# Twelve units of the conditioning matrix at another place in a transformer layer on one core

## The chip, the cores and the metric

The kernel runs on one core of a Trainium2 chip. The metric is the device time of one execution, in microseconds (us). TensorE multiplies matrices, VectorE, ScalarE and GpSimd work element by element, and SyncE's queue starts nearly all transfers from the chip's memory (HBM) to the core's memory (SBUF). In the profile's rows TensorE is PE (PEld its loads of weights), VectorE DVE, ScalarE ACT, GpSimd POOL, and SyncE's queue SPq.

## The reference

One layer of an encoder with three mixers, 256 tokens of 2048 features, in fp32. What matters here is where the conditioning vector enters:

```python
mod = silu(c) @ ada_w + ada_b                       # (2048) @ (2048, 6*2048)
sh1, sc1, gt1, sh2, sc2, gt2 = split(mod, 6)
h = rms(x, norm1_g) * (1 + sc1) + sh1
na.., da.., gd.. = split_cols(h @ w_in)             # inputs of three mixers -> ya, yb, yc
gates = sigmoid(h @ gate_w + gate_b)                # three gates of 2048 columns
merged = gates0 * (ya @ w_branch_a) + gates1 * (yb @ w_branch_b) + gates2 * (yc @ w_branch_c)
x = x + gt1 * (merged @ w_out)
h2 = rms(x, norm2_g) * (1 + sc2) + sh2
x = x + gt2 * ((silu(h2 @ ffn_w1) * (h2 @ ffn_w3)) @ ffn_w2)
```

ya is a neighbourhood attention, yb a differential attention, yc a gated delta rule.

## The kernel before

**The weight stream.** All weights of the large products pass through the core once, as 128x128 tiles in one list that stream_plan writes (line 58). Eight tiles, 128x1024 numbers or 512 KB, are one transfer (load, L929) and are called a half; there are 538 halves. A half is split into a high and a low part of reduced mantissa: ScalarE casts the raw weights to `wh`, and VectorE writes `wl` = raw - wh (conv, L948). The matrix engine then makes wh times both parts of the activations and wl times the high part. The order of the stages is: the input projection, gate A and branch A, gate B with branch B, gate C (halves 194 to 225), branch C, the output projection (from half 242), the feed-forward part (from half 274).

**The units.** mod is computed on VectorE, not on TensorE. Its matrix, transposed, comes in 192 units of 512 KB (ada_units, L254): one transfer into a tile of the pool `raw`, and one scalar_tensor_tensor that multiplies it with silu(c), broadcast in `sb`, and sums along the row into one column of `part`. In the rows a unit's tile is `araw`. Weights and units share the pool `raw` of six buffers, and both kinds of transfer are issued in one order on SyncE's queue. A unit's buffer is free when VectorE has used it, a weight buffer when VectorE has written wl.

**The order of the work.** A loop over the halves (L1154) carries out the units hooked to a half, splits up to two halves ahead (LA = 2), loads up to four ahead, issues the half's matmuls and, after the last one of each tile, advances the side work (the attentions and the delta rule, run_side at L908). Within that order a scheduler of the language's library settles the order of each engine's queue and which buffer a tile gets, when the kernel is built. After the start of the kernel nothing else pins the order on VectorE and ScalarE (`pin` at L153).

**Where the units go.** The first 96 units make shift1 and scale1 and are spread over the input projection. The next 96, called the middle units here, make gate1, shift2 and scale2, 32 for each. They are spread evenly, in order, over three stretches of halves by lines 1129 to 1132, with two borders from line 31:

```python
ADA_AT, ADA_MID = 9, (64, 84)
...
rest = [u for i in range(3) for u in ada_units(ns + i)]
spread(rest[:ADA_MID[0]], first[("ga", ADA_AT)], first[("gc", 0)])
spread(rest[ADA_MID[0]:ADA_MID[1]], first[("gc", 0)], first[("pc", 0)])
spread(rest[ADA_MID[1]:], first[("out", 0)], first[("out", 12)])
```

`first` gives the half in which a group of tiles begins. Worked out from stream_plan these borders are half 132 (the tenth group of gate A), 194, 226, and 242 to 266 of the output projection. The last 32 units (gate2) lie in the feed-forward part.

Of the kernel before, what the change touches and what calls it, by code (L numbers as in the profile page):

```python
# [27 lines left out]
ORDERS = [ALT, [(0, 0), (1, 0), (0, 1), (1, 1)] + ALT[4:], [(0, 0), (0, 1), (1, 1), (1, 0)] + ALT[4:]]  # L28

SHORT = 8  # L30
ADA_AT, ADA_MID = 9, (64, 84)

W = dict(col=4, tok=3, kn=6, s=2, sm=12, sm2=22, pt=5, av=3, gs=21, gt=5, dec=3, prep=3, a=8, x0=9,
         l1=8, l2=6, l3=10, kv=18, uu=6, sw=5, so=6, go=2, conv=2, z=9, sqn=8, pgn=1, sqd=8, pgd=2,
# [1281 lines left out]
```

## Time and profile before

| | us |
|---|---|
| median of 3 runs | 1729.36 (1725.44 to 1732.31) |
| the profiled execution's own time | 1725.35 |
| its span, first to last instruction | 1723.6 |
| TensorE busy in the span | 1697.6 |
| VectorE busy | 1261.2 |
| ScalarE busy | 850.4 |

The span is the part of the execution that the trace shows; the rest, 1.75 us, lies around it. An engine that is busy has an instruction in execution; a matmul's end is modelled in the profile.

### The profile page before, as it was taken

Reading aid. Unit: us, or ns where it says so; the run is one execution under the profiler, and the core shown is the slowest. Engines: PE = TensorE matmul, PEld = TensorE weight load, DVE = VectorE, ACT = ScalarE, POOL = GpSimd, SP = SyncE. Lnnn points to the kernel's source line nnn. Section 1 sums busy time; section 2 is a strip of 40 time slices with the busy share of each in tenths; the row PEclk is TensorE's granted clock in tenths of the full one; section 3 lists DMA queues with packets and bytes.
Section 4 is the critical chain, followed back from the end, with each engine's and each line's share of the span. In section 5 each row is a group of like instructions: output and inputs, shape, how many; then the busy total and the mean of one; then the engine's idle time right before and its main releaser. Section 6 shows DMA issues by size and latency. Waiting matters only on the chain.

```text
span 1723.6 us, 27955 instructions
## 1 busy us (share of the span) xinstructions
PE 1697.6 (98%) x10988; PEld 1531.2 (89%) x10988; DVE 1261.2 (73%) x1895; ACT 850.4 (49%) x1249; POOL 39.1 (2%) x25
## 2 busy tenths in 40 slices
PE   8999999999999999999999999999999999999999
PEld 6999999998889898899898788888888888888887
DVE  6898777986999899876878776666666666545454
ACT  4454455666673445334745554444444444443433
POOL 0000000000003100300000000000000000000000
PEclk9999999999999999999999999999999999999999
DMA  8999964553587775766768567666666666666662
GB/s 326 333 357 324 341 207 156 180 187 128 194 291 237 246 267 195 254 209 214 252 222 278 168 208 227 225 229 224 227 226 229 224 225 226 196 196 202 196 201 96
DMA packets 109432, 393.12 MB, mean 228 GB/s; under 512 B 12146, under 2 KB 14450, under 8 KB 109300
## 3 DMA queue, kind: packets, MB, share of 16 engines
q1 hardware_dynamic: 106852, 389.08, 67.1%
q10 hardware_dynamic: 2448, 2.25, 0.4%
q8 instruction: 86, 1.41, 0.3%
q14 instruction: 46, 0.38, 0.1%
HBM read 389.19 MB, written 2.10 MB: 227 GB/s over the span
## 4 chain that ended last, share of the span: by engine, by line
PE 56%; DVE 1%; DMA 1%; ACT 0%; issue 0%; ACTq 0%; DVEq 0%
PE mm L166 54%; PE sd L166 2%; DMA araw<-ada 1%; DVE wl L157 0%; PE sd L169 0%; ACT wh L157 0%; ACT of L157 0%; DVE araw L157 0%; DVE gc L157 0%; DVE x L157 0%; DVE m L157 0%; DVE po L157 0%; DVE p L157 0%; ACT sq L157 0%; ACT p L157 0%
## 5 line engine op out<-in xcount | busy, mean ns | idle before, releaser
L157 DVE TENSOR_TENSOR wl<-raw,wh 128x1024 fp32r<-128x1024 f32 x538 | 662.8, 1233 | 316.7 <-ACT wh L157 314.1
L157 ACT CAST wh<-raw 128x1024 fp32r<-128x1024 f32 x538 | 563.6, 1048 | 636.1 <-PE mm L166 339.5
L166 PE MATMUL mm<-hp,wh 128*128 128x256 f32 (+1 forms) x2336 | 572.8, 328 | 5.7 <-ACT hp L157 3.2
L166 PE MATMUL mm<-h,wh 128*128 128x512 f32 x1408 | 486.6, 393 | 0.0
L166 PE MATMUL mm<-hp,wl 128*128 128x256 f32 x1552 | 423.3, 282 | 0.0
L166 PEld LDWEIGHTS mm<-hp,wh 128*128 128x128 f32 x2336 | 383.6, 191 | 35.8 <-issue 7.4
L166 PE MATMUL mm<-h,wl 128*128 128x256 f32 x1408 | 387.6, 279 | 0.0
L166 PEld LDWEIGHTS mm<-h,wh 128*128 128x128 f32 x1408 | 261.7, 187 | 57.5 <-DVE sl L157 0.3
L166 PEld LDWEIGHTS mm<-hp,wl 128*128 128x128 f32 x1552 | 295.4, 190 | 12.2 <-issue 3.9
L157 DVE SCALAR_TENSOR_TENSOR araw<-araw,sb 128x1024 f32<-128x1024 f32 x192 | 237.0, 1239 | 86.9 <-DMA araw<-ada 86.3
L166 PEld LDWEIGHTS mm<-h,wl 128*128 128x128 f32 x1408 | 265.1, 188 | 2.6
L166 PE MATMUL mm<-hid,wh 128*128 128x512 f32 x704 | 243.2, 392 | 0.0
L166 PE MATMUL mm<-hid,wl 128*128 128x256 f32 x704 | 193.8, 279 | 0.0
L166 PEld LDWEIGHTS mm<-hid,wh 128*128 128x128 f32 x704 | 130.8, 187 | 28.5
L166 PEld LDWEIGHTS mm<-hid,wl 128*128 128x128 f32 x704 | 132.6, 188 | 1.3
L166 PE MATMUL mm<-m,wh 128*128 128x512 f32 x256 | 89.7, 397 | 0.4 <-DVE po L157 0.3
L166 PE MATMUL mm<-m,wl 128*128 128x256 f32 x256 | 70.8, 280 | 0.0
L166 PEld LDWEIGHTS mm<-m,wh 128*128 128x128 f32 x256 | 47.7, 188 | 12.0 <-DVE po L157 0.6
L758 POOL TENSOR_TENSOR X<-X,of 128x512 f32<-128x512 f32 x20 | 38.4, 1930 | 705.8 <-ACT of L157 705.5
L166 PE MATMUL sd<-hp,wh 128*128 128x256 f32 x256 | 49.5, 283 | 0.0
L166 PEld LDWEIGHTS mm<-m,wl 128*128 128x128 f32 x256 | 48.3, 189 | 0.5
L166 PE MATMUL mm<-yc,wh 128*128 128x256 f32 x256 | 46.2, 283 | 0.0
(251 smaller groups left out, 1521.4 us busy)
## 6 DMA issues: line engine op xcount, KB each, us to landing
raw<-wst SPq DMA_DIRECT2D x538, 512.0 KB, 4.3
araw<-ada SPq DMA_DIRECT2D x192, 512.0 KB, 4.4
x<-xT SPq DMA_DIRECT2D x8, 512.0 KB, 7.1
out<-x ACTq DMA_DIRECT2D x16, 128.0 KB, 3.9
nab<-nab SPq DMA_DIRECT2D x2, 512.0 KB, 6.8
cst<-cst SPq DMA_DIRECT2D x1, 896.0 KB
vec<-vec ACTq DMA_DIRECT2D x1, 152.0 KB, 2.3
lam<-lamv SPq DMA_DIRECT2D x1, 128.0 KB, 3.4
```

The costliest lines, as they stand in the source:

```text
L157: i = f(*a, **k)
L166: return chain("pe", nc.tensor.matmul(*a, **k))
L758: nc.gpsimd.tensor_tensor(sel(X, b), sel(X, b), nat(of[:], b), op=ALU.subtract)
```

## The change

The two borders in the list of the middle units become 52 and 78. The first stretch (halves 132 to 193) has 52 units in place of 64, the third gate (194 to 225) 26 in place of 20, the output projection (242 to 265) 18 in place of 12. Twelve units move later, and every unit keeps its place in the order of units.

```diff
-ADA_AT, ADA_MID = 9, (64, 84)
+ADA_AT, ADA_MID = 9, (52, 78)
```

## Rows read from the trace of the kernel before

**Rows 1.** The page: busy us of each engine, and the group of casts.
```profile
PE 1697.6 (98%) x10988; PEld 1531.2 (89%) x10988; DVE 1261.2 (73%) x1895; ACT 850.4 (49%) x1249; POOL 39.1 (2%) x25
...
L157 ACT CAST wh<-raw 128x1024 fp32r<-128x1024 f32 x538 | 563.6, 1048 | 636.1 <-PE mm L166 339.5
```

**Rows 2.** Busy by stretch: length, PE, PEld, DVE, ACT, POOL, clock, DMA share, GB/s.
```profile
100.00:205.00 105.00, 105.00 (x877) 105.00 (x876) 90.41 (x146) 52.41 (x84) 0.00 (x0) 1.00 0.93 330
435.00:710.00 275.00, 267.74 (x1829) 242.11 (x1828) 253.77 (x397) 143.04 (x229) 28.47 (x14) 1.00 0.72 243
710.00:835.00 125.00, 123.89 (x805) 110.38 (x804) 91.62 (x130) 56.52 (x77) 9.88 (x6) 1.00 0.66 217
883.00:951.00 68.00, 67.55 (x392) 58.76 (x391) 55.99 (x90) 33.61 (x48) 0.00 (x0) 1.00 0.82 270
```

**Rows 3.** Waits of TensorE, 435 to 710 us: us in total, times, longest.
```profile
PE sd L166 <- DVE Y L157: 3.2, 3, 1.7
PE sd L169 <- DVE q L157: 2.4, 1, 2.4
PE sd L169 <- DVE a L157: 1.1, 1, 1.1
```

**Rows 4.** Groups of VectorE, 435 to 710 us: busy, mean ns, idle before.
```profile
L157 DVE SCALAR_TENSOR_TENSOR araw<-araw,sb 128x1024 f32<-128x1024 f32 x64 | 81.1, 1267 | 17.5 <-DMA araw<-ada 17.3
```

**Rows 5.** Groups of VectorE, 710 to 835 us.
```profile
L157 DVE SCALAR_TENSOR_TENSOR araw<-araw,sb 128x1024 f32<-128x1024 f32 x20 | 24.7, 1234 | 19.4 <-DMA araw<-ada 19.3
```

**Rows 6.** Waits of VectorE, 883 to 951 us.
```profile
DVE araw L157 <- DMA araw<-ada: 6.9, 8, 1.2
DVE wl L157 <- ACT wh L157: 5.7, 7, 1.5
```

**Rows 7.** Timeline of SyncE's queue, 900 to 915 us: start, duration.
```profile
908.27 0.33 SPq L260 DMA_DIRECT2D araw<-ada  x1
...
914.21 0.33 SPq L260 DMA_DIRECT2D araw<-ada  x1
```

**Rows 8.** Timeline of VectorE, 900 to 915 us.
```profile
907.01 1.23 DVE L157 SCALAR_TENSOR_TENSOR araw<-araw,sb 128x1024 f32<-128x1024 f32 x1 [0.86 <-DMA araw<-ada]
908.16 0.08 DVE L157 DVE_READ_ACCUMULATOR araw<-araw,sb 128x1 f32 x1
...
912.95 1.23 DVE L157 SCALAR_TENSOR_TENSOR araw<-araw,sb 128x1024 f32<-128x1024 f32 x1 [0.31 <-DMA araw<-ada]
```

**Rows 9.** Timeline of SyncE's queue, 476 to 488 us.
```profile
483.71 0.33 SPq L260 DMA_DIRECT2D araw<-ada  x1
```

**Rows 10.** Timeline of VectorE, 476 to 492 us.
```profile
482.45 1.22 DVE L157 SCALAR_TENSOR_TENSOR araw<-araw,sb 128x1024 f32<-128x1024 f32 x1
...
484.91 1.23 DVE L157 SCALAR_TENSOR_TENSOR araw<-araw,sb 128x1024 f32<-128x1024 f32 x1
...
488.14 1.23 DVE L157 SCALAR_TENSOR_TENSOR araw<-araw,sb 128x1024 f32<-128x1024 f32 x1 [0.86 <-DMA araw<-ada]
```

**Rows 11.** The chain that ended last, 895 to 915 us: start, us, what.
```profile
901.85 5.06 DMA araw<-ada
...
908.24 1.14 DVE wl L157
...
909.76 5.44 PE mm L166 x29
```

**Rows 12.** Groups of VectorE, 100 to 205 us.
```profile
L157 DVE SCALAR_TENSOR_TENSOR araw<-araw,sb 128x1024 f32<-128x1024 f32 x29 | 35.4, 1220 | 0.5 <-DMA araw<-ada 0.5
```

**Rows 13.** Transfers, 100 to 205 us: count, KB each, median us to landing.
```profile
araw<-ada SPq DMA_DIRECT2D x28, 512.0 KB, 5.2
```

**Rows 14.** Transfers, 883 to 951 us.
```profile
araw<-ada SPq DMA_DIRECT2D x11, 512.0 KB, 4.4
```

**Rows 15.** Timeline of VectorE, 949 to 952 and 983 to 986 us.
```profile
950.35 0.17 DVE L157 SCALAR_TENSOR_TENSOR G<-mod,vec 128x16 f32<-128x16 f32 x1
...
984.11 1.27 DVE L157 SCALAR_TENSOR_TENSOR ht<-x,G,rstd 128x256 f32<-128x256 f32 x3
```

## The prediction

> **What bounds the kernel now.** I read first the page's busy times: TensorE works 1697.6 us of a span of 1723.6 us [rows 1]. A change that moves VectorE work and transfers can win only what TensorE stands idle, 26.0 us in all, and only the part of it that lies where work is taken away. So the second view is the busy time by stretch, cut where the change cuts [rows 2]. I took the borders from the order of VectorE's wl writes (one for each block of eight weight tiles, called a half here): the first gates and first two branches (halves 132 to 193) run from 435 to 710 us, the third gate (194 to 225) from 710 to 835 us, and the first 24 halves of the output projection (242 to 265) from 883 to 951 us. TensorE's idle time is 275.00 - 267.74 = 7.26 us in the first, 125.00 - 123.89 = 1.11 us in the second, and 68.00 - 67.55 = 0.45 us in the third. The granted clock is at its upper level (1.00 in the rows, 2.4 GHz) in all of them.
>
> Third, what those idle times wait for. In the first stretch nearly all is TensorE standing at a matmul of the side chains for VectorE's Y, q and a: 3.2 + 2.4 + 1.1 us [rows 3]. VectorE is the engine that is late there: 253.77 us busy and 17.3 us waiting at a unit for its transfer, 98.6% of the 275 us [rows 2, 4]. In the third gate it is 91.62 + 19.3 of 125, 88.7% [rows 2, 5]. In the projection it has 6.9 us of waits for units and 5.7 us for casts [rows 6].
>
> Fourth, how a unit travels, in the queues themselves. In the projection a unit's load is issued at 908.27, just after the unit before it has been used (907.01 + 1.23), and the next again at 914.21, just after 912.95 + 1.23 [rows 7, 8]: one buffer goes round, and a unit costs load plus use. In the first gates, with a unit for nearly every half, two go round: the load at 483.71 follows the use at 482.45 and feeds the use at 488.14, with the one at 484.91 between them [rows 9, 10]. The chain that ended last passes in the projection through such a load (901.85, 5.06 us) and reaches TensorE at 909.76 [rows 11]. So there the units already set the pace at places, with almost no idle time to show for it.
>
> **The change part by part.** A unit is one transfer of 512 KB on SyncE's queue (issue 0.33 us [rows 7]) and one multiply-and-sum on VectorE, 1.22 to 1.27 us, with a read of the accumulator of 0.08 us behind it, beside which the next instruction starts [rows 8]. The change leaves all 192 of them, their order and their deadlines; 12 leave the first gates (64 to 52), 6 more come to the third gate (20 to 26, over 32 halves) and 6 more to the projection (12 to 18, over 24 halves). No work of TensorE, ScalarE or GpSimd is added or removed.
>
> *First gates, a gain.* VectorE loses 12 x (1.267 + 17.3/64) = 18.4 us [rows 4], 6.7 points of 275 us. What TensorE's idle time does with it, I read between the two gate stretches, which have the same kinds of work: 2.64% idle at 98.6% occupation against 0.89% at 88.7%, 0.177 points for one. At 91.9% that is 2.64 - 1.19 = 1.45%, 4.0 us in place of 7.26: **-3.3 us**. The ends are 0 (the stalls are set by the order of the side chains, not by the load) and -7.3 us (all of them go). SyncE's queue has 12 issues less, and the weights' loads behind them come earlier, which nobody waits for.
>
> *Third gate, a small loss.* Six units more are 6 x 1.234 = 7.4 us, 5.9 points, so by the same slope +1.05 points of 125 us: **+1.3 us**. If each new unit also waits as the present ones do (19.3/20 = 0.97 us [rows 5]), it is 13.2 us, 10.6 points, +2.3 us; the lower end is 0, since VectorE waits there 19.3 us at the units themselves and new work could lie in that time. I take 1.3, because a wait for a unit was shorter, 0.27 us, where the units were denser [rows 4]. Behind a waiting unit stand the wl write of the next half and the evacuation of a gate tile; TensorE waits for these only when they are later than the two halves that are split ahead.
>
> *Projection, a loss.* VectorE waits 12.6 us of 68, so 55.4 us are taken [rows 6]. Six units more, at 1.15 us from one start to the next instruction's, are 6.9 us. If each of the 18 waits 6.9/12 = 0.58 us for its transfer as the 12 do now, that is 10.4 us; in all 55.4 + 6.9 + 10.4 = 72.7 us, 4.7 us more than the stretch has. Some of it is lent by the halves split ahead: 392 matmuls in 67.55 us make a half of 16 matmuls 2.76 us [rows 2]; two halves less one cast and one wl write (1.05 and 1.23 us [rows 1]) are 3.2 us. As the chain is already at TensorE in this stretch [rows 11], I count half of that as free: 4.7 - 1.6 = **+3.1 us**. The lower end is 0: from 100 to 205 us the kernel has 29 units in 105 us, one per 3.6 us, as many as the projection would have (18 in the 24 x 2.76 = 66 us of its halves, one per 3.7 us), and VectorE waits only 0.5 us for them and TensorE never stands [rows 2, 12]. The upper end is the rival below, +8.3 us. I take a value between them because the buffer's way round, and not the rate, differs between these stretches, and the order in which the queues are filled after the change is not in this trace.
>
> *Transfers.* 42 loads of 0.524 MB in 66 us are 332 GB/s, against 270 now [rows 2]. From 100 to 205 us the engines moved 330 GB/s, at a share of 0.93, so the rate is to be had. But a unit's load took 5.2 us there against 4.4 us in the projection [rows 13, 14]. The page DMA: Bandwidth & Descriptors of the Trainium skill, section Latency and other measured facts, gives HBM access as 0.2 us on average and 2 us at high load; by it a load would come 1.8 us later, not 0.8, an estimate. The trace bears out the direction and less than half of the size.
>
> *Deadlines.* The last of these units is tied to half 264 before and after, and its vector is made at 950.35 and first used at 984.11 [rows 15], so 34 us are to spare. The gate1 columns are complete at half 162 before and 168 after, and first used at the end of half 249. Neither costs anything.
>
> **Sum.** -3.3 + 1.3 + 3.1 = +1.1 us on the profiled execution's 1725.35 us (its span and 1.75 us around it): 1726.5 us. That execution is 4.0 us below the median of the runs, 1729.36; carried over to it, 1730.5 us.
>
> **The rivals.** *The projection overlaps its loads* as the stretch from 100 to 205 us does: its term is 0 and -3.3 + 1.3 = -2.0 us remain, 1727.4 us; with all of the first gates' stalls gone and no loss, 1722.1. For it speaks that the first gates, with a unit for nearly every half, have two loads in flight [rows 9, 10] and that the stretch from 100 to 205 us hardly waits; against it that the projection, with a unit for every second half, has one [rows 7, 8], and three in four lie between.
>
> *Nothing moves.* TensorE's stalls follow the order of the side chains and the units lie in VectorE's waits everywhere: 1729.4 us.
>
> *Three units in two turns,* the rival of the other sign. Where a unit's load takes the buffer of the unit before it, the next load waits for a wl write that stands behind that unit, and so on: load, use, write, load, use, (4.4 + 1.24) + 1.14 + (4.4 + 1.24) = 12.4 us for three units, while TensorE needs 4 x 2.76 = 11.0 us for the four halves they go with. Six such groups are 6 x 1.4 = +8.3 us in place of 3.1, with the other terms 1735.7 us; with no gain in the first gates and +2.3 us in the third gate, 1740. For it: the round of one buffer in rows 7 and 8. It decides (over 8.6 us in all) from the point where every one of these groups chains and the first gates give nothing back.
>
> *Loads slowed by the higher rate.* With one buffer going round, 0.8 us longer loads add 18 x 0.8 = 14.4 us to VectorE's waits, 3.1 + 14.4 = 17.5 us in the projection: 1744.9 us. By the 1.8 us worked out from that page of the Trainium skill, as an estimate, the term would be 35.5 us and the time 1763 us. If all 18 units went round one buffer, the stretch would need 18 x 5.64 = 101.5 us 35.3 us more than those halves, 33.7 us with the free half of the lead: 1761 us. Against both: at 330 GB/s and 5.2 us per load TensorE did not stand at all [rows 2, 13].
>
> **How the numbers follow.** The forecast gets 0.42, overlap 0.30, nothing moves 0.09, two turns 0.12, slowed loads or a single round 0.07. I predict 1730.5 us. From 1723 to 1740 us the range holds the forecast with its bounds, overlap and nearly all of the two turns, and leaves out the tail of overlap below 1723 and the last case. About 0.5%, 8.6 us, is what a measurement of this kernel tells from no change. Faster than that needs more than the 7.26 us that TensorE stands in the first gates: 0.05, for a new order of the queues that also helps elsewhere. Slower: the last case and half of the two turns, 0.13. The rest, 0.82, is within 0.5%.
>
> **What the profile after would show.** Right: TensorE's idle time between 435 and 710 us falls to about 4 us with fewer waits for Y, q and a; that of the third gate stays within some 2.5 us; in the projection TensorE stands some 3 us for wl writes or evacuations, VectorE waits about 0.6 us for a unit, and the load of a unit is issued just after the use of the one before it. If the load follows the use of the one before the last, overlap has won, and the projection has no idle time. Loads of over 5 us beside idle time of over 10 us would be the last rival. If the idle time of the first gates doesn't fall, the slope between the two stretches was no measure. The prediction would also be wrong if the filling of the queues changes so far that a stretch which the change doesn't touch, as the feed-forward part after 1000 us, gets idle time.

## The result and the profile after

The changed kernel takes 1741.01 us (median of 4 runs, 1738.76 to 1743.26) against 1730.28 us for the kernel before (4 runs). The ratio is 1.0062 [1.0048, 1.0076], +10.7 us with 8.3 to 13.1: slower by 0.6%, clear of the noise. The prediction, 1730.5 us within 0.5% and at most 1740, was 10.5 us too low, and the time lies just above its range.

The profiled execution after took 1738.76 us. It has to be read beside two executions of before: the one of the prediction (1725.35 us), the fastest of its runs, and a second one taken later, b_again (1731.66 us), which is near the median. The page after, busy times and the group of units:

```profile
PE 1704.3 (98%) x10988; PEld 1537.5 (89%) x10988; DVE 1257.3 (72%) x1895; ACT 852.7 (49%) x1249; POOL 32.8 (2%) x25
...
L157 DVE SCALAR_TENSOR_TENSOR araw<-araw,sb 128x1024 f32<-128x1024 f32 x192 | 237.0, 1239 | 112.3 <-DMA araw<-ada 111.8
```

The span is 1737.0 us, so TensorE stands 32.7 us, against 26.0 in [rows 1]; its busy time has risen too, by 6.7 us, for the same 10988 matmuls. Both halves of the loss need an explanation. The windows after, cut at the same halves as [rows 2], and under them stretches of 3 and 4 us (length, PE, PEld, DVE, ACT, POOL, clock, DMA share, GB/s):

```profile
436.00:713.00 277.00, 268.33 (x1821) 243.76 (x1820) 239.49 (x377) 143.94 (x230) 22.45 (x14) 0.99 0.67 221
713.00:844.00 131.00, 128.24 (x829) 113.70 (x828) 97.33 (x141) 57.79 (x79) 9.58 (x6) 1.00 0.69 228
891.00:965.00 74.00, 70.84 (x403) 61.57 (x402) 62.77 (x99) 33.38 (x48) 0.00 (x0) 0.98 0.86 288
...
485.00:489.00 4.00, 3.41 (x13) 3.05 (x14) 3.15 (x7) 1.77 (x5) 0.00 (x0) 0.57 0.83 292
680.00:684.00 4.00, 4.00 (x21) 3.86 (x21) 4.00 (x5) 1.32 (x2) 0.00 (x0) 0.57 0.38 132
922.00:926.00 4.00, 4.00 (x16) 3.45 (x15) 3.69 (x7) 1.36 (x4) 0.00 (x0) 0.57 0.81 270
486.00:489.00 3.00, 3.00 (x13) 2.61 (x12) 2.15 (x4) 1.77 (x5) 0.00 (x0) 0.51 0.77 254
```

The first stretch has lost 14.3 us of VectorE's work (253.77 to 239.49) and still stands 8.67 us. The third gate stands 2.76 us, the projection 3.16. The last four lines show what raised the busy time: for a few microseconds the granted clock is at its lower level (0.51, 1.2 GHz), and 4 x (1 - 0.57) = 1.7 us of clock are lost each time, three times inside the changed stretches. Before each of the three TensorE had just stood for about 2 to 2.7 us. Its waits in the three stretches (us in total, times, longest):

```profile
PE sd L169 <- DVE a L157: 2.7, 1, 2.7
PE sd L169 <- DVE q L157: 2.5, 1, 2.5
PE sd L166 <- DVE Y L157: 2.4, 3, 1.1
...
PE sd L166 <- DVE uu L157: 1.6, 1, 1.6
PE mm L166 <- DVE wl L157: 1.2, 2, 0.8
...
PE mm L166 <- DVE po L157: 2.0, 1, 2.0
PE mm L166 <- DVE gc L157: 1.2, 1, 1.2
```

Y, q and a are those of [rows 3]: Y has fallen from 3.2 to 2.4 us, a has risen from 1.1 to 2.7. In the third gate it is a matmul of the delta rule that waits for `uu`, in the projection a matmul that waits for `gc`, the end of branch C, and later one that waits for the evacuation `po`. The first two lower-clock stretches follow the stalls for a and q, the third that for po. VectorE's waits at the units, the same three stretches:

```profile
L157 DVE SCALAR_TENSOR_TENSOR araw<-araw,sb 128x1024 f32<-128x1024 f32 x53 | 67.6, 1275 | 28.3 <-DMA araw<-ada 28.0
...
L157 DVE SCALAR_TENSOR_TENSOR araw<-araw,sb 128x1024 f32<-128x1024 f32 x25 | 30.8, 1232 | 32.4 <-DMA araw<-ada 32.4
...
L157 DVE SCALAR_TENSOR_TENSOR araw<-araw,sb 128x1024 f32<-128x1024 f32 x18 | 22.0, 1223 | 8.7 <-DMA araw<-ada 8.7
```

Fewer units in the first gates wait longer: 28.0 us for 53, against 17.3 for 64 [rows 4]. In the third gate a unit waits 1.30 us on average against 0.97 [rows 5]. In the projection it is 0.48, less than the 0.58 that the prediction took over from before.

One place in the third gate shows how a unit reaches TensorE. VectorE's timeline after, 799 to 808 us (start, duration, idle time before):

```profile
803.63 1.23 DVE L157 SCALAR_TENSOR_TENSOR araw<-araw,sb 128x1024 f32<-128x1024 f32 x1 [3.15 <-DMA araw<-ada]
...
805.12 1.22 DVE L157 TENSOR_TENSOR wl<-raw,wh 128x1024 fp32r<-128x1024 f32 x1
806.25 1.28 DVE L157 TENSOR_TENSOR uu<-uu,sd 128x512 f32<-128x512 f32 x2
```

and TensorE's:

```profile
806.99 0.49 PE L166 MATMUL sd<-kq,uu 128*128 128x128 f32 x2 [1.55 <-DVE uu L157]
```

The unit waits 3.15 us for its transfer; the gate's evacuation, a wl write and `uu` are queued behind it on VectorE, and the delta rule's next matmul, which waits for `uu`, stops TensorE for 1.55 us. VectorE is idle for those 3.15 us although work stood ready: ScalarE had written the evacuation's input, gc, by 800.2, and VectorE's part of it started at 804.78, after the unit.

In the projection SyncE's queue after reads, 936 to 950 us:

```profile
943.17 0.33 SPq L260 DMA_DIRECT2D araw<-ada  x1
...
946.95 0.33 SPq L260 DMA_DIRECT2D araw<-ada  x1
```

and VectorE's timeline there:

```profile
940.40 1.23 DVE L157 SCALAR_TENSOR_TENSOR araw<-araw,sb 128x1024 f32<-128x1024 f32 x1 [0.19 <-DMA araw<-ada]
...
945.69 1.23 DVE L157 SCALAR_TENSOR_TENSOR araw<-araw,sb 128x1024 f32<-128x1024 f32 x1 [0.34 <-DMA araw<-ada]
...
948.30 1.22 DVE L157 SCALAR_TENSOR_TENSOR araw<-araw,sb 128x1024 f32<-128x1024 f32 x1
```

The load at 943.17 follows the use at 940.40 and feeds the one at 948.30, with 945.69 between: two loads are in flight, where before one buffer went round [rows 7, 8]. So the overlap that the first rival named did come for most units, and the projection lost time all the same. Not for all: of the 18 loads that feed its units, three were issued just after the use of the unit before, as in [rows 7, 8], and the longest wait stands behind one of them. SyncE's queue, VectorE and TensorE at that place:

```profile
913.76 0.33 SPq L260 DMA_DIRECT2D araw<-ada  x1
...
912.50 1.23 DVE L157 SCALAR_TENSOR_TENSOR araw<-araw,sb 128x1024 f32<-128x1024 f32 x1 [0.89 <-DMA araw<-ada]
...
918.52 1.22 DVE L157 SCALAR_TENSOR_TENSOR araw<-araw,sb 128x1024 f32<-128x1024 f32 x1 [2.51 <-DMA araw<-ada]
...
920.81 0.74 DVE L157 TENSOR_TENSOR po<-po,mm 128x256 f32<-128x256 f32 x2
...
921.28 0.49 PE L166 MATMUL mm<-m,wh 128*128 128x512 f32 x1 [1.98 <-DVE po L157]
```

The load at 913.76 follows the use at 912.50, its unit waits 2.51 us, `po` comes behind the unit, TensorE stands 1.98 us, and the clock falls: one buffer's round, as the prediction had it.

The second execution of before, for comparison; windows of the same halves, then two short ones:

```profile
436.00:714.00 278.00, 268.25 (x1817) 243.55 (x1817) 255.14 (x397) 143.87 (x228) 28.43 (x14) 0.99 0.72 240
714.00:841.00 127.00, 126.17 (x821) 112.39 (x819) 93.38 (x133) 57.50 (x78) 9.88 (x6) 1.00 0.65 215
888.00:957.00 69.00, 68.02 (x402) 59.70 (x401) 56.44 (x90) 33.40 (x48) 0.00 (x0) 1.00 0.80 268
...
580.00:584.00 4.00, 3.45 (x16) 3.35 (x17) 4.00 (x7) 0.00 (x0) 0.00 (x0) 0.57 0.73 254
682.00:686.00 4.00, 4.00 (x23) 3.86 (x21) 4.00 (x5) 1.32 (x2) 0.00 (x0) 0.59 0.40 127
```

It too has the lower clock for some microseconds, twice in the first gates (0.57, 0.59), and stands 9.75 us there where the first trace stood 7.26. Cut at the matmuls where each product begins and ends, its stages and those of after last: first gates with branches A and B 277.7 and 276.0 us, third gate 125.4 and 127.7, branch C 47.2 and 49.3, projection 90.6 and 95.2. The differences, -1.7 + 2.3 + 2.1 + 4.6 = +7.3 us, are nearly the 7.1 us by which the spans differ (1729.9 and 1737.0). The mean clock over the span was 0.999 in the first trace of before, 0.995 in the second and 0.994 after: 1.7, 8.6 and 10.4 us of clock.

These differences have to be read beside the scatter. The order of VectorE's instructions in a trace can be compared with that of before. It is the same through the third gate and branch C in e3_out and e11_work_out below, and there the third gate took 128.3 and 127.4 us with its 20 units, so that four traces of equal order lie between 125.4 and 128.3: the 2.3 us of the third gate are within that, and so are the 1.7 us of the first gates (273.5 to 278.5 in seven traces of equal order). The 49.3 us of branch C (47.0 to 47.7 in the four) and the 95.2 us of the projection (90.3 to 91.2 in four of equal order) are outside.

### The profile page after: what moved, and what is told of

It is laid out like the page before. It is cut to its first block, busy times and chain, and to the rows that moved or that the text cites. A ratio compares the mean times of both kernels' runs of the same rounds, so it can differ in the third digit from the quotient of the medians.

```text
span 1737.0 us, 27948 instructions
## 1 busy us (share of the span) xinstructions
PE 1704.3 (98%) x10988; PEld 1537.5 (89%) x10988; DVE 1257.3 (72%) x1895; ACT 852.7 (49%) x1249; POOL 32.8 (2%) x25
## 4 chain that ended last, share of the span: by engine, by line
PE 54%; DVE 2%; DMA 2%; issue 1%; ACT 0%; DVEq 0%; ACTq 0%
PE mm L166 52%; PE sd L166 2%; DMA araw<-ada 2%; DVE wl L157 1%; PE sd L169 0%; DVE araw L157 0%; ACT wh L157 0%; DVE go L157 0%; DVE gc L157 0%; DVE yc L157 0%; ACT L183 0%; ACT yc L157 0%; DVE kk L157 0%; DVE vb L157 0%; DVE x L157 0%
## 5 line engine op out<-in xcount | busy, mean ns | idle before, releaser
L166 PEld LDWEIGHTS mm<-hp,wl 128*128 128x128 f32 x1552 | 296.5, 191 | 14.2 <-issue 3.9
L758 POOL TENSOR_TENSOR X<-X,of 128x512 f32<-128x512 f32 x20 | 32.0, 1610 | 714.1 <-ACT of L157 611.0
```

The source lines that it names most:

```text
L166: return chain("pe", nc.tensor.matmul(*a, **k))
L758: nc.gpsimd.tensor_tensor(sel(X, b), sel(X, b), nat(of[:], b), op=ALU.subtract)
```

## The experiments

Three explanations stood against each other. By *occupation*, a unit costs TensorE what VectorE's busy share in its stretch makes it cost, so taking some away must win time. By *rounds*, what counts is how many loads are in flight: fewer units in the first gates go round one buffer, wait longer, and eat the gain. By *order*, the stalls hang on where q, Y, a, uu, po stand in VectorE's queue behind a unit, so removed work wins no time and added work is paid for. Differences in microseconds below are the ratio less 1, times about 1730 us. "Second pass" is a further multiply of a unit's tile by itself on VectorE, 1.2 to 1.3 us, that changes no value.

**The first gates alone.** e1_first: 52 units in the first gates, 20 and 12 after them as before; 12 units of scale2 are left out, their columns set to zero.

```diff
-ADA_AT, ADA_MID = 9, (64, 84)
+ADA_AT, ADA_MID = 9, (52, 72)
...
+    V.memset(part, 0.0)
...
+    rest = rest[:83] + rest[95:]
```

> Only the first part: 52 units in the first gates, 20 and 12 in the other two stretches as before; the 12 units between are left out (their part of scale2 is taken as zero). Load theory (VectorE's load sets TensorE's stalls, as the prediction had it): about 3.3 us less than the kernel before, 1727, and less waiting of VectorE for units than its 17.3 us there. Round theory (with gaps between units the loads go round one buffer, each waiting for the use of the unit before): no gain, 0 to 3 us more than before, 1730 to 1733, and 24 us or more of waits for units between 435 and 710 us.

Measured: 1731.41 us (11 runs) against 1729.63; 1.0012 [1.0001, 1.0023], +2.1 us where -3.3 was predicted. Its window, its units and its waits in that stretch:

```profile
437.00:714.00 277.00, 267.66 (x1805) 242.73 (x1804) 237.38 (x373) 143.03 (x228) 23.91 (x14) 0.98 0.66 221
...
L157 DVE SCALAR_TENSOR_TENSOR araw<-araw,sb 128x1024 f32<-128x1024 f32 x53 | 67.2, 1269 | 28.8 <-DMA araw<-ada 28.8
...
PE sd L169 <- DVE q L157: 3.3, 1, 3.3
PE sd L169 <- DVE a L157: 2.7, 1, 2.7
```

With nothing added anywhere the stretch stands 9.3 us. The stall for a is 2.7 us as in the changed kernel, and 1.1 in both traces of before. It goes with the order of VectorE's queue: with the units taken out, that order in the first gates is the same in e1_first and in the changed kernel, and it differs at 46 of 260 instructions from before. No run changes this order and nothing else.

**Work or loads.** Two kernels take away one of the two. e13_loads_kept keeps all 64 loads and takes the multiply-and-sum from 12 of them (those columns of mod are zero; a copy of 8 columns holds the buffer). e14_work_kept has the 52 units of e1_first (12 left out) and gives 12 of them a second pass.

```diff
+            if mode[0] == 1:          # e13: 12 of the first 64
+                V.tensor_copy(raw[:, 0:8], raw[:, 8:16])
+                return
...
+            if mode[0] == 2:          # e14: 12 of the first 52
+                stt(raw, raw, 1.0, raw, op0=ALU.mult, op1=ALU.max)
```

> The kernel before (64, 20, 12) in which 12 of the 64 units of the first gates are only loaded, and VectorE moves 8 of their columns in place of the sum (their part of mod is left out): VectorE loses 15 us of work there and the loads stay. Load theory: 3.3 us less than before, 1726.5, since TensorE's stalls there follow VectorE's occupation. Round theory: the same gain, as the alternation of loads stays; that the 12 units left out entirely gave none was the fault of the sparser loads. If neither, and the stalls hang on the order of the side chains alone: within 1.5 us of before.

> As the first experiment (52, 20, 12, twelve units left out), with 12 of the 52 making a second pass on VectorE: the loads of 52 units, the work of 64. Load theory: 3.3 us more than without the second passes, 1734.5. Round theory: VectorE's waits for loads take the second passes in part, +1 to +3. Order of the side chains alone: within 1.5 us of the first experiment, 1730 to 1733.

Measured: e13 1729.71 us, e14 1729.72 (11 runs each), against 1729.36; 1.0001 [0.9989, 1.0012] and 0.9996 [0.9985, 1.0008]. The unit rows of e13, then of e14:

```profile
L157 DVE SCALAR_TENSOR_TENSOR araw<-araw,sb 128x1024 f32<-128x1024 f32 x52 | 64.4, 1238 | 23.2 <-DMA araw<-ada 23.2
```

```profile
L157 DVE SCALAR_TENSOR_TENSOR araw<-araw,sb 128x1024 f32<-128x1024 f32 x53 | 67.9, 1281 | 14.7 <-DMA araw<-ada 14.7
L157 DVE SCALAR_TENSOR_TENSOR araw<-araw 128x1024 f32<-128x1024 f32 x12 | 15.7, 1307 | 0.0
```

Taking away 12 sums or 12 loads wins no time that can be measured. That speaks against occupation for removals, and against rounds as the reason: e13 has the loads of before, and the gain is missing just the same. The order of VectorE's other instructions changed here too (at 18 of 260 in e13, 51 in e14). In e14 the 15.7 us of second passes lie in the waits for units, which fall from 28.8 us to 14.7.

The clock hides a small gain, though. The mean granted clock of the runs of e1, e13 and e14 is 0.9947, 0.9959 and 0.9962, that of the kernel before beside them 0.9969. Taken as time of the span, this is 3.7, 1.6 and 1.2 us more lost to the clock; without it the three would be some 1.5 to 2 us shorter than before. This is an estimate, since the record gives the clock of a run to 0.001, 1.7 us. So a part of the predicted gain may have been there, and the lower clock took it back.

**More in the first gates,** the change the other way: e15_more_first has 76, 14 and 6 units.

```diff
-ADA_AT, ADA_MID = 9, (64, 84)
+ADA_AT, ADA_MID = 9, (76, 90)
```

> The opposite of the change: 76, 14 and 6 units. Load theory, the predicted terms turned round: +3.3 - 1.3 - 3.1, 1.1 us less than before. If the stretches stand at a knee, where units taken away give nothing and units added cost about 1 us each: up to 1.2 us won in the third gate and the projection, 5 to 12 us lost in the first gates, 1734 to 1741.

Measured: 1738.09 us against 1729.36; 1.0051 [1.0036, 1.0065], +8.8 us. Its window and waits in the first gates:

```profile
437.00:724.00 287.00, 272.82 (x1829) 246.87 (x1828) 269.66 (x420) 142.98 (x228) 27.34 (x14) 0.98 0.74 253
...
PE sd L166 <- DVE Y L157: 5.7, 7, 2.3
PE sd L169 <- DVE q L157: 5.1, 2, 2.8
PE sd L169 <- DVE a L157: 3.0, 1, 3.0
```

TensorE stands 14.2 us, and VectorE is busy or waits at a unit for 269.66 + 9.2 of 287 us. So the kernel before stands at a knee: 12 units less there win no time, 12 more cost 8.8 us, net of what the third gate and the projection give back with 14 and 6.

**The third gate alone.** e2_third repeats six of its units there (26 in all, none taken from elsewhere, nothing changed in the values). e6_work_third gives six of its 20 units a second pass; e10_loads_third adds six loads with a copy of 8 columns and no sum.

```diff
+    spread(rest[64:84] + rest[64:70], first[("gc", 0)], first[("pc", 0)])        # e2
...
+    spread([second(u) if i in (1, 4, 7, 11, 14, 17) else u for i, u in enumerate(rest[64:84])], ...)  # e6
...
+        nc.sync.dma_start(raw, ada[apos[32 + j], 0])                             # e10
+        V.tensor_copy(raw[:, 0:8], raw[:, 8:16])
```

> Only the second part: 64, 26 and 12 units; six units of the third gate are carried out twice with the same result. Load theory: +1.3 us on the kernel before, 1731.5. Round theory: the third gate goes round one buffer already, six more turns of some 5.2 us in 125 us leave VectorE late, the side chain ends late before branch C and TensorE stands there: +4 to +6 us, 1734 to 1736.

> The kernel before (64, 20, 12), in which six units of the third gate make a second pass over their tile on VectorE (no result changed): VectorE's share of six units without their loads. Load theory: as much as six units more cost there, +5 to +9 us (1735 to 1738). Round theory: the loads and their waits make the cost, not the 7 us of work: 0 to +2 us (1730 to 1732).

> The kernel before (64, 20, 12) with six loads more in the third gate: each brings a unit's tile into a raw buffer and VectorE moves 8 of its columns, without the sum over it. Six whole units more cost about 7 us there and the six sums alone about 3. If loads and sums add up: +3 to +5 us on the kernel before, 1733 to 1735. If only the sums count: 0 to +1 us. If only the rounds of the buffer count: +6 us or more, 1736.

Measured: e2 1736.66 us against 1729.63, 1.0051 [1.0039, 1.0063], +8.8 us; e6 1733.55 against 1731.02, 1.0024 [1.0014, 1.0033], +4.2; e10 1733.45 against 1729.56, 1.0024 [1.0013, 1.0035], +4.2. Six units cost 1.5 us each, about half by the sum on VectorE and half by the load, and within their intervals the halves add up. The load's half is not the transfer alone: in e10 the six copies wait 14.4 us on VectorE for their tiles. In e2 the longest wait of the stretch is the same one as after:

```profile
PE sd L166 <- DVE uu L157: 2.1, 1, 2.1
```

**The projection alone.** e3_out repeats six of its units (18 in all); e11_work_out gives six of its 12 a second pass.

```diff
+    spread(rest[84:95] + rest[84:90] + rest[95:], first[("out", 0)], first[("out", 12)])      # e3
...
+    spread([second(u) if i % 2 else u for i, u in enumerate(rest[84:])], ...)                 # e11
```

> Only the third part: 64, 20 and 18 units; six units of the output projection are carried out twice with the same result. Load theory as predicted: +3.1 us, 1733.5, with VectorE waiting about 0.6 us for each unit. Round theory: the same denser units get two loads in flight, waits for units stay near 10 us in all; the loss then is VectorE's work alone and one stretch of lower clock, +3 to +5 us.

> The kernel before (64, 20, 12) in which six of the projection's twelve units make a second pass over their tile on VectorE: the work of six units more, without loads. Six whole units more cost about 5 us there. If VectorE's work is the cost: +4 to +6 us, 1734 to 1736. If the loads are, 0 to +1.5 us, 1730 to 1732.

Measured: e3 1735.09 us against 1729.63, 1.0038 [1.0025, 1.005], +6.6 us; e11 1732.33 against 1729.56, 1.0013 [1.0000, 1.0026], +2.2 (0 to 4.5). In e3's trace TensorE stands for gc (1.4 us) and po (1.2 us) at the same two places as after. The work is about a third of the cost; that the loads are the rest, some 4 us, is a difference of two runs, since loads alone were not run here.

**The placing in the first gates.** e7_first_dense is the changed kernel with its 52 units one to a half in halves 132 to 183, so that the loads overlap as before.

```diff
+    spread(rest[:ADA_MID[0]], first[("ga", ADA_AT)], first[("ga", ADA_AT)] + ADA_MID[0])
```

> The changed kernel (52, 26, 18) with the 52 units of the first gates put one to each half from 132 to 183, without the ten gaps. Round theory: the alternation of unit and weight keeps two units in flight, waits for units between 435 and 705 us fall from 26 to 18 us or less, and the first gates' stalls of 2.7 and 2.5 us shrink: 2 to 5 us less than the changed kernel, 1736 to 1739. Load theory: the same units closer together make the stalls before half 184 larger: 1741 or more.

Measured: 1738.08 us against 1731.02; 1.0043 [1.003, 1.0055]. VectorE's waits for units in the first gates fell from 28.0 to 24.1 us in its trace, and the stretch took 275.7 us against 276.0. The interval of the time overlaps that of the changed kernel: what the sparser placing costs, if anything, is not settled by it.

**Buffers for the units alone.** e4_after_4_2 is the changed kernel with four buffers for weights and two for units; e9_after_5_2 has five and two, and one page less in the pool of pages (NPAGE, 30).

```diff
-    rawp = pool("raw", 6)
+    rawp = pool("raw", 4)          # e9: 5, and NPAGE 30
+    arawp = pool("araw", 2)
...
-            raw = rawp.tile([P, 1024], F32, tag="raw", name=nm("araw"))
+            raw = arawp.tile([P, 1024], F32, tag="araw", name=nm("araw"))
```

> The changed kernel (52, 26, 18) with the six raw buffers divided: four for weights, two for units alone, so that two units' loads can be in flight everywhere. Round theory: waits for units between 435 and 835 us fall from 59 us to under 25, and the time from 1741 to 1730 or below. Load theory: the same work on VectorE, so the time stays within 3 us of 1741; with only four weight buffers it could be longer.

> The changed kernel with seven raw buffers, five for weights and two for units alone, and one page of the pool of pages less (30). Round theory: two units in flight everywhere and the weights as far ahead as before: waits for units between 435 and 845 us under 30 us against 60, 1727 to 1733. Load theory: within 3 us of 1741.

Measured: 1758.94 and 1758.13 us, 1.0174 [1.0161, 1.0187] and 1.0157 [1.0143, 1.017]. TensorE has long stalls far from the change, at 39 us (6.0 us in e9) and 55 us (3.7 us), where it waits for ScalarE's `hp`, a split part of the activations; that fewer buffers for weights are behind this is likely and not shown. Half 132 comes 26.1 and 18.3 us later than in the changed kernel's trace, the last half 27.0 and 18.6: nearly all of the loss is there before the middle units begin. From half 132 to branch C the waits for units are half, 32.5 and 30.1 us against 60.3, as was hoped, and nothing is won by it. But the weights have fewer buffers at the same time, so this doesn't separate the two.

**Units where VectorE has room.** In halves 66 to 131, before the first gates, TensorE never stands and VectorE is busy 198.90 of 245 us in the kernel before:

```profile
195.00:440.00 245.00, 245.00 (x1826) 231.17 (x1825) 198.90 (x359) 143.79 (x230) 0.00 (x0) 1.00 0.55 185
```

v1_early_48 puts 48 of the 96 middle units there and 48 into the first gates, none later; v2_early_32 puts 32 and 64.

```diff
+    spread(rest[:48], first[("in", 2, 0)] + ADA_OVER + 3, first[("ga", ADA_AT)])     # v2: 32
+    spread(rest[48:], first[("ga", ADA_AT)], first[("gc", 0)])
...
```

> All middle units before the third gate: 48 spread over halves 66 to 131, where there are none now and TensorE never stands, and 48 over halves 132 to 193. If units cost where VectorE is full and not where it has room, the third gate and the projection lose their waits: 2 to 5 us less than before, 1725 to 1728. If the sparse first gates go round one buffer as in the change, that gain is given back: 1730.

> As the one above, with 32 units over halves 66 to 131 and 64 over halves 132 to 193 as before, none later. The first gates keep their order of alternating loads: 1 to 4 us less than before, 1726 to 1729. If the gain in the third gate and the projection is only their idle time of some 2 us, no difference that can be measured.

Measured: 1748.9 and 1743.35 us against 1729.56; 1.0113 [1.0092, 1.0134] and 1.0077 [1.0059, 1.0096]. The same matmuls in v1_early_48:

```profile
195.00:468.00 273.00, 255.68 (x1830) 236.00 (x1829) 248.52 (x455) 144.96 (x231) 0.00 (x0) 0.98 0.77 258
...
PE mm L166 <- DVE wl L157: 9.3, 15, 1.1
PE sd L169 <- DVE s L157: 5.1, 3, 3.6
```

49.6 us more of VectorE's work lengthen the stretch by 28 us, and TensorE stands for wl and the side chains. That is more work than the 46 us that VectorE had without work, so this run alone doesn't show that they were no room; v2_early_32 does. In its trace:

```profile
223.00:460.00 237.00, 228.07 (x1618) 210.92 (x1618) 212.98 (x397) 133.98 (x217) 0.00 (x0) 0.98 0.66 224
```

Halves 66 to 131 take 219.0 us in the trace of before, VectorE busy for 179.3 of them, and 236.4 us here: some 34 us more work, less than the 39.7 us that stood free, and 17.4 us longer. The third gate, branch C and the projection, with no unit left in them, gave back 2.1 us (261.1 against 263.2 in b_again). The first gates, with 48 units and another order ahead of them, took 270.0 us in this trace against 277.7, with 5.6 us of standing and no lower clock; in v2_early_32, with 64, it was 275.2. The 270.0 is outside the 273.5 to 278.5 us of the seven traces with 64 units there: a gain from 16 units less may be had in another order, but it comes from one trace and was not run by itself. The Trainium skill (Perfetto Trace Analysis, section Identifying the Most-Contended Engine) calls the occupancy of VectorE a fair measure of how close it is to roofline. What TensorE would lose or win could not be read from it here: at 82% (179.3 of 219.0 us) work that fitted into the idle time cost 17.4 us, and at 92% (253.77 of 275 us [rows 2]) a reduction won no time.

No kernel that was run beats the one before.

**The same kernel again.** b_again is the kernel before, for a second trace.

> The kernel before once more, for a second trace: which of its stalls and of the lower-clock stretches come back. If the stretches of lower clock near 48 and 99 us, which the changed kernel shows before anything is changed, belong to single executions, some appear here too; the stalls of TensorE at 481, 520, 575 and 674 us should come back within 0.5 us.

Measured: 1731.66 us; its windows stand above. The lower clock near 48 and 99 us is in it too. Of the four stalls the one for a came back at 1.1 us, those for Y and q longer (2.2 for 1.7 us, 2.7 for 2.4), and two new ones of 1.0 and 1.2 us stand between them, in the same order of VectorE's queue.

## Why the prediction was wrong, point by point

**First gates, -3.3 us: the step that failed.** The prediction took "what TensorE's idle time does" from the slope between two gate stretches, 0.177 points for one. No removal bears it out in time: sums, loads and whole units taken from this place gave 0, 0 and +2.1 us. By the estimate from the clocks of these runs, some 1.5 to 2 us of standing may have gone, and the lower clock, which the prediction had at 1.00, took back 1.2 to 3.7. The idle time did not fall to 4 us but is 8.67, and the prediction had said what that would mean: the slope was no measure. The lower end it had kept, 0 because "the stalls are set by the order of the side chains", fits the time. That order moved with the units: TensorE waits 2.7 us for a in the changed kernel and in e1_first, whose first 52 units are placed alike, and 1.1 us in both traces of before. How far this holds for larger removals is open (v1_early_48).

**Third gate, +1.3 us: mis-sized.** The mechanism, VectorE late behind a unit, is right and shown at 803 to 807 us. In the changed kernel's trace the stretch is 2.3 us longer, no more than traces of equal order differ, and branch C another 2.1: 4.4 us together, above the upper end of 2.3. The size rests on the timed run with that part alone, which gave 8.8 (6.7 to 10.9). Two things were left out: the sum takes in VectorE's busy time and not where the wait stands in its queue, and it stops at the stretch's border. In branch C TensorE stands 1.0 us for `yc`, the delta rule's result, and in neither trace of before for it; the rest of the 2.1 is not placed.

**Projection, +3.1 us: right in sign, too small.** It is 4.6 us in the trace and 6.6 (4.3 to 8.6) alone, inside the range of the term. Its reason held at one place and not as a sum. A unit waits 0.48 us on average, 8.7 us in all where 10.4 were put in, two loads are in flight for most units, and the load takes 4.6 us, hardly more than the 4.4 of [rows 14], at 288 GB/s: by the first rival this term was 0. The cost came from two single waits, 1.2 us for gc at the start of the projection and 2.0 us for po at 921 us, and from the lower clock after the second, 1.7 us. The wait for po stands behind a unit whose load went round one buffer, as predicted; that for gc stands behind a unit that did not wait. The sum spread such waits evenly and set the lead of two halves, half of it counted as free, against them; single waits went past it. It also dropped VectorE's 5.7 us of waits for casts [rows 6] without a reason; 3.3 us of them are there after. On the load time the Trainium skill's 2 us of HBM access at high load (DMA: Bandwidth & Descriptors, section Latency and other measured facts) was again not seen; the rise here is 0.2 us.

**The clock: left out.** The prediction read 1.00 in all stretches and took it as given. After stalls of 2 to 2.7 us it was 0.57 over 4 us, 1.7 us of clock each time, so that a stall costs up to nearly twice its length. By the mean clock this is 10.4 us of the execution after and 8.6 of the second one before, but that one lost more than most of its kind. The 78 executions of the kernel before on record with a clock have a mean of 0.9968, which is 5.5 us, and the four after 0.994 (0.992 to 0.997), 10.4 us. So some 5 us of the 10.7, an estimate from four runs, are lower clock, a term that the prediction put at nothing. The Trainium skill (TensorE: Matmul & The Clock Gate, section A second HAM failure mode: psum-queue depth-cycling) says that short idle times between groups of matmuls can make the clock swing between its two levels; these rows agree in that the clock fell after stalls as short as 2.0 us.

**The base.** The profiled execution had a mean clock of 0.999 and was the fastest of its runs. Its stalls in the first gates were 2.5 us short of those in the second trace (7.26 against 9.75). The shift of 4.0 us to the median corrected the time but not these rows, from which the slope was made.

**The rivals.** "Nothing moves" was right of the first gates alone. "Three units in two turns" gave the sign and nearly the size (1735.7 to 1740), but not by its mechanism: in the projection three single loads of 18 went round one buffer, no two of them in a row, where six groups of three had been counted. "Slowed loads" did not come. Deadlines were met, as predicted.

**The sum.** With 0 for the first gates and the +4.4 and +4.6 us of the changed kernel's own trace it would have been +9.0; +10.7 was measured. By this trace the gain that never came (3.3 us) and the third gate with branch C (3.1) are the largest errors, by the runs of one part alone the third gate (7.5).

**Still open.** The parts timed alone, 2.1 + 8.8 + 6.6 = 17.5 us, are more than the whole, 10.7 (8.3 to 13.1). They aren't the same thing: e2 and e3 add repeated units beside a full first stretch. In the trace of e2 its third gate and branch C are only 3.2 and 1.0 us longer than in b_again; stages of equal order differ by 2 to 3 us from one execution to the next, so that a single trace can't place the rest. Why they differ, and why a stall of one length brings the lower clock in one execution and not in another, was not found.

## What to carry to other kernels

An engine that feeds the bound one may have no room where it is idle: here VectorE waited at one instruction with the urgent ones behind it. So test a slope by adding and by removing at the same place before a sum rests on it; here removing 12 units won no time and adding cost 0.7 us (12 units, first gates) to 1.5 us (six, third gate) for each unit of 1.2 us. And take a second trace of the kernel before, with the clock in short windows, and compare the mean clock of all runs: the fastest execution showed fewer stalls than the second one, and the clock took back what the removals may have won.

## What was not expected of the hardware

TensorE's granted clock falls to 0.51 to 0.59 for some microseconds inside stretches in which it is busy 96 to 97%, after stalls of 2.0 to 2.7 us. Six loads with a copy of 8 columns in place of the sum cost 4.2 us (2.2 to 6.1) in the third gate, where the transfer engines were busy only 0.66 of the time [rows 2] and 0.68 with them; the price seems to lie in what waits for a load rather than in its share of the bandwidth, which no run tests apart.
